# A hybrid decoder step: splitting a mixer's input weights one layer part earlier, and a state update of the decode tokens by matrix products

## The chip, the core and the metric

The kernel runs on one core of one Trainium2 chip. The time is the device time of one execution in microseconds (us); the figure to compare is the median of several executions. The engines are named as in the profile: PE is TensorE (matrix products, with PEld for its weight loads), DVE is VectorE, ACT is ScalarE, POOL is GpSimd, and SP is the sync engine, which here does nothing but issue transfers. Each engine works through its own instructions in a fixed order; a transfer that waits on SP holds up every transfer behind it.

## The reference

A prompt of 1024 new tokens and 8 decode tokens (one new token for each of 8 running sequences) go through two layers. Both sets use the same weights, so the kernel treats them as one block of T = 1032 columns. Layer 0 mixes with a gated DeltaNet and a retention head group, layer 1 with a Mamba-2 (SSD) mixer; each is followed by a squared-ReLU MLP.

```python
for layer in range(DEPTH):                       # DEPTH = 2
    h = rms_norm(x, norm_mix[layer])
    out, states = mixer(h, ...)                  # layer 0: hybrid, layer 1: ssd_mixer
    x = x + out
    a = relu(rms_norm(x, norm_mlp[layer]) @ mlp_w1[layer])      # 1024 -> 4096
    x = x + (a * a) @ mlp_w2[layer]                             # 4096 -> 1024

# ssd_mixer: z, xbc, dt = split(h @ w_in)        # w_in: 1024 x 5152
# xbc = silu(causal_conv(xbc)); xs, B, C = split(xbc)
# 4 groups of 8 heads, head width 64, state size 128, per head and token:
#     S = exp(dt * a) * S + outer(B, dt * xs)     # S: 128 x 64
#     y = S.T @ C + d * xs
```

For the prompt the recurrence is evaluated in blocks. For a decode token it is one step: 8 tokens x 32 heads, each with its own 128 x 64 state, which is read from memory, updated and written back.

## The kernel before

**Products in three passes.** All large products are made in the round-to-fp32r format: each fp32 operand is split into a high part, rounded to fp32r, and the low rest, and `mm3` adds up three products: high weight by high input (line 150), high weight by low input (line 151), low weight by high input (line 152). The input's parts lie in SBUF as `xh`, `xl` (8 tiles of 128 x 1032 each). The weights come as fp32 and are split on the way. `load_w` does it for a piece of 128 x 512: a transfer on SP's queue into `raw` (line 136, three buffers in turn), the norm weight multiplied in on POOL (line 140, `raw<-raw,vec`), the high part by a cast on ACT (line 144, `whi`), the low part by a subtraction on DVE or POOL (line 145, `wlo`). The two parts go to a ring of six buffers, so three pieces are ready or in use at a time.

**A gemm tile** (`products`, `gemm_units`) makes 128 output rows for all 1032 columns: two pieces ("halves"), each used by 3 column blocks of 344 x 4 input tiles x 3 passes = 36 products. The three results are evicted by DVE. A step of the MLP's second product (`gemm_flush`) also uses one piece with 36 products.

**The stages.** The layer-0 mixer and its output projection fill about 0 to 800 us, the first MLP about 800 to 1540, the SSD mixer to about 2330, its output projection, and the second MLP to the end. In an MLP, `up(t)` runs 32 times (one gemm tile each), and after every fourth one `down(b)` adds 4 hidden tiles into the output: eight steps, one for each 128 output rows.

**The SSD mixer** needs 40 gemm tiles of the input weights `wis`: per group 6 that go through the causal convolution (DVE lines 409 to 413, ACT) and 4 gates. While the recurrence of group g runs (`ssd_group`), the gates of group g-1 and the tiles of group g+1 are interleaved. DVE carries evictions, convolution, half of the low parts, and the recurrence; the PSUM tiles of the recurrence (`ps`, two buffers, and `pm`, three) come free when DVE has read them.

**The decode step** (`ssd_decode`, lines 1693 to 1754) holds the state with (head, width) on the partitions and the state size along the free dimension. Per token: ACT scales the four 128 x 128 parts of the state (line 1744), DVE adds a broadcast row B times a per-partition scalar (line 1746, four instructions), POOL multiplies by the broadcast row C (line 1749), DVE reduces (line 1750). PE only broadcasts the rows B and C for two tokens at a time (line 1737, two products of 256 columns), and helps in the preparation (lines 1705, 1720). States come in two at a time on SP's queue (line 1729).

**What sets the order.** The program is written as nested generators; a scheduler then orders each engine's instructions from that, so an instruction can stand ahead of one that is written before it.

## Time and profile before

| | |
|---|---|
| median of 3 executions | 3213.82 us (3210.69 to 3222.39) |
| profiled execution, its own time | 3203.04 us |
| its span, first to last instruction | 3200.8 us |
| PE busy | 3052.8 us, 95% |
| DVE, ACT, POOL busy | 54%, 26%, 39% |
| mean granted PE clock | 0.973 |

The profile gives the busy time of each engine, in total or by windows; the groups of instructions by line, with the mean duration of one and the idle time before them; the waits of an engine with what ended them; and the single instructions in order of time. Two things need care. A PE product is listed with its whole passage, some 320 ns for 344 columns, but the next one starts about 160 ns after it, so durations on PE overlap, and what one costs is read from start to start. And a full fp32 product is listed as two.

### The profile page before, as it was taken

What the parts mean: (1) busy time and instruction counts of PE and PEld (TensorE: products, weight loads), DVE (VectorE), ACT (ScalarE), POOL (GpSimd) and SP (SyncE); (2) the same over time, 40 slices, a digit from 0 to 9 for tenths busy, and PEclk for the clock granted to TensorE, in tenths of its full rate; (3) what the DMA queues carried; (4) which work ended last, traced back from release to release, by engine and by line L of the source; (5) the groups of instructions that cost most, each with busy time, mean ns of one, the idle gap of its engine ahead of it and who ended that gap; (6) DMA issues with size and microseconds to landing.
All of it is one profiled execution on the core that took longest, in us unless ns stands there. A gap on an engine that the chain in (4) does not pass through costs nothing. (4 is left out here: it accounts for less than half of the span.)

```text
span 3200.8 us, 49506 instructions
## 1 busy us (share of the span) xinstructions
PE 3052.8 (95%) x19758; PEld 2918.4 (91%) x19758; DVE 1724.0 (54%) x3189; ACT 841.2 (26%) x1604; POOL 1264.1 (39%) x1234
## 2 busy tenths in 40 slices
PE   7999999989999999999998999999899999999998
PEld 6888888879999999999987988897899999999998
DVE  7664767464333333335888696978635333333334
ACT  3221222214111111114344434343214111111112
POOL 4332324146323323335246556556625233232224
PEclk8899999889999999999999999999999999999999
DMA  3011103133111111111112121222531111111112
GB/s 122 23 44 59 47 22 105 42 132 116 47 47 47 47 48 48 48 47 46 42 52 65 50 84 58 80 74 96 186 109 44 50 47 47 47 47 47 47 49 71
DMA packets 102326, 202.14 MB, mean 63 GB/s; under 512 B 12624, under 2 KB 27728, under 8 KB 102096
## 3 DMA queue, kind: packets, MB, share of 16 engines
q1 hardware_dynamic: 94800, 173.82, 17.4%
q0 software_dynamic: 7296, 25.17, 2.0%
q8 instruction: 155, 2.54, 0.3%
q14 instruction: 75, 0.61, 0.1%
HBM read 157.94 MB, written 38.89 MB: 61 GB/s over the span
## 5 line engine op out<-in xcount | busy, mean ns | idle before, releaser
L150 PE MATMUL pg<-xh,whi 128*128 128x344 f32 x3072 | 1003.2, 327 | 10.8 <-DVE sxc L1460 4.8
L151 PE MATMUL pg<-xl,whi 128*128 128x344 f32 x3072 | 998.2, 325 | 0.0
L152 PE MATMUL pg<-xh,wlo 128*128 128x344 f32 x3072 | 997.2, 325 | 0.7 <-DVE wlo L145 0.7
L150 PEld LDWEIGHTS pg<-xh,whi 128*128 128x128 f32 x3072 | 585.5, 191 | 18.4 <-DVE sxc L1460 5.8
L144 ACT CAST whi<-raw 128x512 fp32r<-128x512 f32 (+2 forms) x443 | 271.6, 613 | 1257.9 <-PE pg L151 859.2
L152 PEld LDWEIGHTS pg<-xh,wlo 128*128 128x128 f32 x3072 | 585.2, 191 | 4.5 <-issue 1.7
L151 PEld LDWEIGHTS pg<-xl,whi 128*128 128x128 f32 x3072 | 584.2, 190 | 4.8 <-issue 2.8
L140 POOL TENSOR_TENSOR raw<-raw,vec 128x512 f32<-128x512 f32 x264 | 306.2, 1161 | 636.8 <-DMA raw<-w 330.0
L151 PE MATMUL pg<-alo,whi 128*128 128x344 f32 (+2 forms) x1476 | 472.4, 320 | 0.0
L152 PE MATMUL pg<-ahi,wlo 128*128 128x344 f32 (+2 forms) x1476 | 472.3, 320 | 0.0
L150 PE MATMUL pg<-ahi,whi 128*128 128x344 f32 (+2 forms) x1476 | 471.5, 319 | 0.0
L1236 DVE TENSOR_TENSOR acc<-acc,pg 128x344 f32<-128x344 f32 x360 | 183.1, 512 | 385.0 <-PE pg L152 384.7
L145 POOL TENSOR_TENSOR wlo<-raw,whi 128x512 fp32r<-128x512 f32 (+2 forms) x179 | 225.2, 1260 | 328.4 <-ACT whi L144 327.4
L145 DVE TENSOR_TENSOR wlo<-raw,whi 128x512 fp32r<-128x512 f32 x264 | 198.4, 752 | 195.6 <-ACT whi L144 185.8
L1227 POOL TENSOR_TENSOR r<-r 128x344 f32<-128x344 f32 x192 | 146.1, 762 | 386.0 <-ACT ahi L1226 337.3
L152 PEld LDWEIGHTS pg<-ahi,wlo 128*128 128x128 f32 x1476 | 277.6, 188 | 0.0
L150 PEld LDWEIGHTS pg<-ahi,whi 128*128 128x128 f32 x1476 | 277.5, 188 | 0.0
L151 PEld LDWEIGHTS pg<-alo,whi 128*128 128x128 f32 x1476 | 277.3, 188 | 0.0
L1228 DVE TENSOR_TENSOR alo<-r,ahi 128x344 fp32r<-128x344 f32 x192 | 135.5, 707 | 254.1 <-POOL r L1227 254.1
L1226 ACT ACTIVATE ahi<-r 128x344 fp32r<-128x344 f32 x192 | 94.7, 493 | 338.8 <-DVE r L1225 338.8
L1225 DVE SCALAR_TENSOR_TENSOR r<-pg,rstd_bc 128x344 f32<-128x344 f32 x186 | 94.9, 510 | 76.7 <-PE pg L152 75.4
L150 PE MATMUL pg<-mhi,whi 128*128 128x344 f32 x408 | 131.5, 323 | 4.9 <-DVE acc L1342 4.9
(540 smaller groups left out, 4439.8 us busy)
## 6 DMA issues: line engine op xcount, KB each, us to landing
raw<-w SPq DMA_DIRECT2D x256, 256.0 KB, 2.6
raw<-wis SPq DMA_DIRECT2D x80, 256.0 KB, 2.7
raw<-wih SPq DMA_DIRECT2D x56, 256.0 KB, 2.9
mraw<-spill SPq DMA_DIRECT2D x17, 512.0 KB, 4.1
accd<-ost SPq DMA_DIRECT2D x48, 172.0 KB, 2.5
acc<-accd SPq DMA_DIRECT2D x16, 516.0 KB, 6.9
dS<-sstate SPq DMA_DIRECT2D x32, 256.0 KB, 2.7
o_sssm<-dS POOLq DMA_DIRECT2D x32, 256.0 KB, 2.3
```

The costliest lines, as they stand in the source:

```text
L140: (norm_eng or nc.gpsimd).tensor_tensor(out=r3, in0=r3, in1=normw.unsqueeze(2).to_broadcast([P, k, n // k]), op=ALU.mult)
L144: nc.scalar.copy(hi[:, :n], raw[:, :n])
L145: (lo_eng or nc.vector).tensor_tensor(out=lo[:, :n], in0=raw[:, :n], in1=hi[:, :n].bitcast(F32), op=ALU.subtract)
L150: t.matmul(ps, lhsT=whi, rhs=xhi, start=start, stop=False)
L151: t.matmul(ps, lhsT=whi, rhs=xlo, start=False, stop=False)
L152: t.matmul(ps, lhsT=wlo, rhs=xhi, start=False, stop=stop)
L1225: nc.vector.scalar_tensor_tensor(out=r, in0=ps, scalar=0.0, in1=self.rstd_bc[:, s], op0=ALU.max, op1=ALU.mult)
L1226: nc.scalar.activation(hi[:, s], r, AF.Square)
L1227: nc.gpsimd.tensor_tensor(out=r, in0=r, in1=r, op=ALU.mult)
L1228: nc.vector.tensor_tensor(out=lo[:, s], in0=r, in1=hi[:, s].bitcast(F32), op=ALU.subtract)
L1236: nc.vector.tensor_tensor(out=s, in0=s, in1=ps, op=ALU.add)
```

## The change

Three parts.

1. **`presplit`**: during the first MLP, the 80 pieces of `wis` are loaded into the `raw` ring, multiplied by the norm weight (POOL, line 164 of the changed kernel), split into `phi` (ACT) and `plo` (DVE) in four buffers of their own, and both parts are written to a buffer in device memory (`split`, 40 x 128 x 4 x 512, line 169). It is a generator: one piece after each `up`, one after each of the first seven steps of each `down`. All `raw` tiles share one ring of three, the presplit's among them.
2. **`load_half`** with a tile number as source: in the SSD mixer the two parts of a half are fetched as they are, by two transfers straight into the `hl` ring (line 176); no engine touches them.
3. **The decode step** keeps the state as (state size) x (head, width). The tokens' values and B rows are transposed to 8 partitions each and laid out in parts (high, high, low against high, low, high) on partitions 0, 32 and 64 of `sxr` and `sbst`; `dBm` masks B by token for four tokens at a time. Per token: POOL scales the state by a factor broadcast beforehand (`egb`), PE makes the outer product in one fp32r product of 512 columns (line 1774), DVE adds it (line 1775), and four full-fp32 products with the state as weights and one column of C give the output (line 1778). ACT copies two tokens' outputs.

The packing of `state_ssm` and the unpacking of its output on the host follow the new layout.

```diff
@@ load_half, presplit
+    def presplit(self, tp):
+        nc, I = self.nc, self.I
+        normw = self.V("mix1", 0, 8)
+        for i in range(40):
+            for kh in range(2):
+                raw = self.wp.tile([P, 512], F32, tag="raw", name="praw", bufs=RAWB)
+                nc.sync.dma_start(raw, I["wis"][i][:, kh * 512:kh * 512 + 512])
+                r3 = raw.rearrange("p (k c) -> p k c", k=4)
+                nc.gpsimd.tensor_tensor(out=r3, in0=r3, in1=normw[...].to_broadcast([P, 4, 128]), op=ALU.mult)
+                hi, lo = [tp.tile([P, 512], F32R, tag="phl", name=nm, bufs=4) for nm in ("phi", "plo")]
+                nc.scalar.copy(hi, raw)
+                nc.vector.tensor_tensor(out=lo, in0=raw, in1=hi.bitcast(F32), op=ALU.subtract)
+                for s, x in enumerate((hi, lo)):
+                    nc.sync.dma_start(self.split[i][:, kh * 2 + s], x.bitcast(F32))
+                yield
     def load_half(self, src, kh, M, normw):
+        if isinstance(src, int):
+            hl = [self.wp.tile([P, 512], F32R, tag="hl", name=nm, bufs=6) for nm in ("whi", "wlo")]
+            for s, x in enumerate(hl):
+                self.nc.sync.dma_start(x.bitcast(F32), self.split[src][:, kh * 2 + s])
+            return hl
@@ mlp
+            pre = iter(()) if last else self.presplit(tp)
...
                 self.gemm_tile(I["w1"][l, t], 128, normw, ev, t == 1)
+                next(pre, None)
...
-                for _ in self.gemm_flush(lambda m: I["w2"][l, b, m], [parts.pop(k) for k in ks], ev):
-                    pass
+                for m, _ in enumerate(self.gemm_flush(lambda m: I["w2"][l, b, m], [parts.pop(k) for k in ks], ev)):
+                    if m < 7:
+                        next(pre, None)
@@ ssd_decode, per pair of tokens
-            pb = self.pm()
             for j in range(2):
-                t.matmul(pb[:, j * 256:j * 256 + 256], lhsT=st["sel8"][...].to_broadcast([16, P]), rhs=rows, start=True, stop=True)
-            bc = small("bc", [P, 2, 2, 128])
-            a.copy(bc, pb.rearrange("p (b k n) -> p b k n", b=2, k=2))
-            for j in range(2):
...
+                gs.tensor_tensor(out=s3, in0=s3, in1=st["egb"][:, b, hs].unsqueeze(2).to_broadcast([P, 8, 64]), op=ALU.mult)
+                po = self.pm()
+                t.matmul(po, lhsT=Bm[:, b % 4], rhs=xr, start=True, stop=True)
+                v.tensor_tensor(out=s, in0=s, in1=po, op=ALU.add)
+                nc.gpsimd.dma_start(self.O["sssm"][g, b], s)
                 for i in range(4):
-                    a.activation(s[:, i], s[:, i], AF.Copy, scale=egf[:, i, b:b + 1])
-                for i in range(4):
-                    v.scalar_tensor_tensor(out=s[:, i], in0=bc[:, j, 0], scalar=xd[:, i, b:b + 1], in1=s[:, i], op0=ALU.mult, op1=ALU.add)
-                nc.gpsimd.dma_start(self.O["sssm"][g, b], cur[j])
-                pr = half("dpr").rearrange("p (i n) -> p i n", i=4)
-                gs.tensor_tensor(out=pr, in0=s, in1=bc[:, j, 1].unsqueeze(1).to_broadcast([P, 4, 128]), op=ALU.mult)
-                v.tensor_reduce(out=y[:, :, b], in_=pr, axis=AX.X, op=ALU.add)
+                    t.matmul(py[:, i * 2 + j:i * 2 + j + 1], lhsT=s[:, i * 128:i * 128 + 128], rhs=C[:, SEQ + b:SEQ + b + 1], start=True, stop=True)
+            a.copy(y[:, :, b0:b0 + 2], py[:, 0:8].rearrange("p (i k) -> p i k", i=4))
```

**The order on SP in the first MLP.** Before, at the passage from the fourth `up` to the first `down`, SP issues the weight pieces one behind the other (line 136 loads; `w1`, `w2` are the MLP's weights):

```order
L136 DMA raw_8140<-w1 128x512
L136 DMA raw_8198<-w2 128x512
L136 DMA raw_8246<-w2 128x512
L136 DMA raw_8294<-w2 128x512
L136 DMA raw_8342<-w2 128x512
L136 DMA raw_8390<-w2 128x512
```

In the changed kernel, in the same `down`, a presplit load (`praw`, line 162) and two writes (line 169, to `split`) stand around every weight piece (line 137):

```order
L162 DMA praw_8447<-wis 128x512
L169 DMA split3_92<-phi_8450 128x512
L169 DMA split3_92<-plo_8451 128x512
L137 DMA raw_8456<-w2 128x512
L162 DMA praw_8504<-wis 128x512
L137 DMA raw_8513<-w2 128x512
L169 DMA split4_93<-phi_8507 128x512
L169 DMA split4_93<-plo_8508 128x512
L162 DMA praw_8561<-wis 128x512
L137 DMA raw_8570<-w2 128x512
```

The writes of a piece stand right behind its own load, so SP waits there until POOL, ACT and DVE have made the parts, and the next weight piece is behind that wait.

**The order on PE at the first pair of decode tokens.** Before, after the last product of a gemm tile come the two broadcasts of line 1737, and the next tile follows (lines 150 to 152):

```order
L152 MATMUL pg_15600<-xh7_78,wlo_15648 128x344
L1737 MATMUL pm_15709<-drows_15589,sel8_14290 128x256 x2
L150 MATMUL pg_15740<-xh0_71,whi_15746 128x344
L151 MATMUL pg_15740<-xl0_79,whi_15746 128x344
L152 MATMUL pg_15740<-xh0_71,wlo_15747 128x344
L150 MATMUL pg_15740<-xh1_72,whi_15746 128x344
```

In the changed kernel (its gemm lines are 151 to 153) the outer product of the first token stands there, then eight gemm products, then the four one-column products of that token and the outer product of the second:

```order
L1774 MATMUL pm_16415<-sxr_15347,dBm_16411 128x512
L151 MATMUL pg_16435<-xh0_71,whi_16438 128x344
L152 MATMUL pg_16435<-xl0_79,whi_16438 128x344
L153 MATMUL pg_16435<-xh0_71,wlo_16439 128x344
L151 MATMUL pg_16435<-xh1_72,whi_16438 128x344
L152 MATMUL pg_16435<-xl1_80,whi_16438 128x344
L153 MATMUL pg_16435<-xh1_72,wlo_16439 128x344
L151 MATMUL pg_16435<-xh2_73,whi_16438 128x344
L152 MATMUL pg_16435<-xl2_81,whi_16438 128x344
L1778 MATMUL pm_16413<-bc_15788,dS_16300 128x1 x4
L1774 MATMUL pm_16424<-sxr_15347,dBm_16411 128x512
L153 MATMUL pg_16435<-xh2_73,wlo_16439 128x344
```

Line 1778 waits for DVE's sum of line 1775, which waits for the product of line 1774; eight gemm products now stand between the two.

**The order on DVE at the same place.** Before, DVE has the low part of a weight piece (line 145), and the decode's line 1746 in between the convolution of the next group (lines 409 to 413):

```order
L1460 TENSOR_TENSOR sxc_15596<-pg_15600,rstd_bc_70 128x344
L145 TENSOR_TENSOR wlo_15972<-raw_15968,whi_15971 128x512
L409 TENSOR_SCALAR x_15240<-sxc_15596,scwh_14286 128x8
L1746 SCALAR_TENSOR_TENSOR dS_15592<-dbc_15712,dxd_15576,dS_15592 128x128
L413 SCALAR_TENSOR_TENSOR x_15240<-sst_15237,scwh_14286,x_15240 128x8
L1746 SCALAR_TENSOR_TENSOR dS_15592<-dbc_15712,dxd_15576,dS_15592 128x128
L413 SCALAR_TENSOR_TENSOR x_15240<-sst_15237,scwh_14286,x_15240 128x8
L1746 SCALAR_TENSOR_TENSOR dS_15592<-dbc_15712,dxd_15576,dS_15592 128x128
L411 SCALAR_TENSOR_TENSOR x_15240<-sxc_15596,scwh_14286,x_15240 128x1024
L413 SCALAR_TENSOR_TENSOR x_15240<-sst_15237,scwh_14286,x_15240 128x8
L411 SCALAR_TENSOR_TENSOR x_15240<-sxc_15596,scwh_14286,x_15240 128x1024
L1746 SCALAR_TENSOR_TENSOR dS_15592<-dbc_15712,dxd_15576,dS_15592 128x128
```

In the changed kernel (convolution lines 432 to 436, evictions line 1495) the low parts are gone and one sum per token, line 1775, is left:

```order
L1495 TENSOR_TENSOR sxc_16304<-pg_16307,rstd_bc_70 128x344
L1495 TENSOR_TENSOR sxc_16304<-pg_16308,rstd_bc_70 128x344
L1775 TENSOR_TENSOR dS_16300<-dS_16300,pm_16415 128x512
L432 TENSOR_SCALAR x_15969<-sxc_16304,scwh_15048 128x8
L436 SCALAR_TENSOR_TENSOR x_15969<-sst_15966,scwh_15048,x_15969 128x8 x2
L1775 TENSOR_TENSOR dS_16302<-dS_16302,pm_16424 128x512
L434 SCALAR_TENSOR_TENSOR x_15969<-sxc_16304,scwh_15048,x_15969 128x1024
L436 SCALAR_TENSOR_TENSOR x_15969<-sst_15966,scwh_15048,x_15969 128x8
L434 SCALAR_TENSOR_TENSOR x_15969<-sxc_16304,scwh_15048,x_15969 128x1024 x2
```

The sum stands right behind the eviction of the gemm tile that ends just before the outer product.

More of the change, by code (lines that the diff above doesn't have):

```diff
@@ L134, in load_w @@
         nc = self.nc
-        raw = self.wp.tile([P, 512], F32, tag="raw", name="raw", bufs=3)
+        raw = self.wp.tile([P, 512], F32, tag="raw", name="raw", bufs=RAWB)
         nc.sync.dma_start(raw[:, :n], src)
@@ L1324, in mlp @@
                 down(HID // 4 - 1)
+                for _ in pre:
+                    pass
                 self.rstd = self.rstd_from()
@@ L1380, in ssm_setup @@
         self.first = self.others()
-        for u, _ in enumerate(self.products(I["wis"][4], 128, normw, self.first)):
+        for u, _ in enumerate(self.products(4, 128, normw, self.first)):
             if u == 1:
@@ L1440, in ssm_setup @@
         nc.vector.tensor_scalar(out=nsel, in0=sel.bitcast(F32), scalar1=-1.0, scalar2=None, op0=ALU.mult)
+        bg = gp.tile([8, 8, 32], F32, tag="hf", name="sbg", bufs=SHF)
+        nc.vector.tensor_tensor(out=bg, in0=g[:8, 8, :].unsqueeze(1).to_broadcast([8, 8, 32]),
+                                in1=self.ident[:8, :8].unsqueeze(2).to_broadcast([8, 8, 32]), op=ALU.mult)
         pt = self.pm()
-        nc.tensor.transpose(pt[:32, 0:8], dt[:8, 8, :], self.ident[:8, :8])
-        nc.tensor.transpose(pt[:32, 8:16], g[:8, 8, :], self.ident[:8, :8])
-        dg = gp.tile([32, 16], F32, name="dgd")
-        nc.scalar.copy(dg, pt[:32, 0:16])
-        st.update(dt=dt, gc=gc, kdf=kdf, egend=egend, grow=grow, sel=sel, nsel=nsel, idr=idr, mmr=mmr, sel8=sel8, dg=dg)
+        nc.tensor.matmul(pt[:, 0:256], lhsT=self.ones[:8, :], rhs=bg.rearrange("p b h -> p (b h)"), start=True, stop=True)
+        egb = gp.tile([P, 8, 32], F32, name="segb")
+        nc.scalar.activation(egb.rearrange("p b h -> p (b h)"), pt[:, 0:256], AF.Exp)
+        xr = gp.tile([P, 512], F32R, name="sxr")
+        bst = gp.tile([P, 128], F32R, name="sbst")
+        for r, n in ((xr, 4), (bst, 1)):
+            nc.vector.tensor_scalar(out=r.rearrange("p (c k) -> p c k", c=n), in0=self.U.unsqueeze(1).to_broadcast([P, n, 128]),
+                                    scalar1=0.0, scalar2=None, op0=ALU.mult)
+        st.update(dt=dt, gc=gc, kdf=kdf, egend=egend, grow=grow, sel=sel, nsel=nsel, idr=idr, mmr=mmr, seq=c3, egb=egb, xr=xr, bst=bst)
         return st
@@ L1595, in ssd_group @@
         selg = selg.rearrange("p h k -> p (h k)")
-        dec = self.ssd_decode(gp, g, x, B, C, st, half, selg)
+        dec = self.ssd_decode(gp, g, x, B, C, st, half)
         grow = st["grow"]
@@ L1691, in ssd_group, with ssd_decode @@
         nc.gpsimd.dma_start(self.O["pssm"][g], S)
-    def ssd_decode(self, gp, g, x, B, C, st, half, selg):
+    def ssd_decode(self, gp, g, x, B, C, st, half):
         nc = self.nc
@@ L1697, in ssd_decode @@
         ident = self.ident
+        hs = slice(g * 8, g * 8 + 8)
         dec = slice(SEQ, T)
-        def small(name, sh, dt=F32):
-            return gp.tile(sh, dt, tag="d" + name, name="d" + name, bufs=1)
-        pd = self.pm()
+        xr, bst = st["xr"], st["bst"]
+        pt = self.pm()
         for i in range(4):
-            t.matmul(pd[:, i * 16:i * 16 + 16], lhsT=selg[:32, i * 128:i * 128 + 128].bitcast(F32), rhs=st["dg"], start=True, stop=True)
-        pd3 = pd[:, 0:64].rearrange("p (i k) -> p i k", i=4)
-        dtf, egf = small("dtf", [P, 4, 8]), small("egf", [P, 4, 8])
-        a.copy(dtf, pd3[:, :, 0:8])
-        a.activation(egf, pd3[:, :, 8:16], AF.Exp)
-        xd = small("xd", [P, 4, 8])
-        v.tensor_tensor(out=xd, in0=x[:, :, dec], in1=dtf, op=ALU.mult)
-        hi, parts = small("hi", [P, 2, 8], F32R), small("parts", [P, 2, 16])
-        for k, src in enumerate((B[:, dec], C[:, dec])):
-            v.tensor_copy(hi[:, k], src)
-            v.tensor_copy(parts[:, k, 0:8], hi[:, k].bitcast(F32))
-            v.tensor_tensor(out=parts[:, k, 8:16], in0=src, in1=hi[:, k].bitcast(F32), op=ALU.subtract)
-        pt = self.pm()
-        for k in range(2):
-            t.transpose(pt[:16, k * 128:k * 128 + 128], parts[:, k], ident)
-        rows = small("rows", [16, 256], F32R)
-        a.copy(rows, pt[:16, 0:256])
-        y = small("y", [P, 4, 8])
+            t.transpose(pt[:8, i * 128:i * 128 + 128], x[:, i, dec], ident)
+        xd = half("dxd")[:8]
+        v.tensor_tensor(out=xd.rearrange("p (h k) -> p h k", h=8), in0=pt[:8].rearrange("p (h k) -> p h k", h=8),
+                        in1=st["dt"][:8, 8, hs].unsqueeze(2).to_broadcast([8, 8, 64]), op=ALU.mult)
+        a.copy(xr[0:8], xd)
+        a.copy(xr[32:40], xd)
+        v.tensor_tensor(out=xr[64:72], in0=xd, in1=xr[0:8].bitcast(F32), op=ALU.subtract)
+        pt = self.pm()
+        t.transpose(pt[:8, 0:128], B[:, dec], ident)
+        a.copy(bst[0:8], pt[:8, 0:128])
+        a.copy(bst[64:72], pt[:8, 0:128])
+        v.tensor_tensor(out=bst[32:40], in0=pt[:8, 0:128], in1=bst[0:8].bitcast(F32), op=ALU.subtract)
+        y = gp.tile([P, 4, 8], F32, tag="dy", name="dy", bufs=1)
         def fetch(b0):
@@ L1759, in build @@
         k = Kern(ctx, tc, I, O)
+        sp = ctx.enter_context(tc.tile_pool(name="split", bufs=1, space=bass.MemoryType.DRAM))
+        k.split = [sp.tile([P, 4, 512], F32, name=f"split{i}") for i in range(40)]
         k.layer(0)
```

28 lines of the change are left out of this document (16 added, 12 removed).

## The prediction

> **What bounds the kernel now.** I read the page's first lines, then busy time by windows cut at the stages, then PE's waits inside the SSD mixer. A windows row has the stretch, its length, the busy time of PE, PEld, DVE, ACT and POOL with the instruction counts, the granted clock, the DMA share and GB/s.
>
> ```profile
> PE 3052.8 (95%) x19758; PEld 2918.4 (91%) x19758; DVE 1724.0 (54%) x3189; ACT 841.2 (26%) x1604; POOL 1264.1 (39%) x1234
> 800.00:1460.00 660.00, 660.00 (x4197) 660.00 (x4196) 230.00 (x411) 117.76 (x208) 203.22 (x207) 1.00 0.16 47
> 1540.00:2330.00 790.00, 732.01 (x4816) 675.55 (x4816) 613.09 (x976) 297.61 (x563) 433.19 (x365) 0.98 0.25 83
> ```
>
> In the first MLP (800 to 1460) PE never pauses, and DVE, POOL and ACT are busy for 35%, 31% and 18%. In the SSD mixer (1540 to 2330) PE is idle for 790 - 732 = 58 us, DVE is busy for 613 of 790 us (78%), POOL for 55%. So work can be taken to the first MLP under cover, and all that removing it from the mixer can win is those 58 us and what the granted clock lost. These are PE's longest waits in the mixer (in total, times, longest):
>
> ```profile
> PE ps L1677 <- DVE x L1667: 10.6, 10, 2.2
> PE ps L1665 <- DVE yi L1674: 9.8, 6, 3.0
> PE pg L150 <- DVE ost L473: 5.6, 4, 2.8
> PE pm L1645 <- DVE selg L1594: 5.2, 1, 5.2
> PE pg L150 <- DVE sxc L1460: 4.8, 4, 1.9
> PE pg L150 <- DVE z L1485: 4.5, 2, 2.5
> PE pg L150 <- DVE acc L1342: 3.2, 1, 3.2
> PE ps L294 <- DVE dg L292: 2.3, 4, 0.7
> ```
>
> Every one ends with DVE: PE is the bound and DVE is what makes it pause. `ost`, `acc` and `dg` (11.1 us) belong to the norms and the output projection, which the change leaves alone. That leaves 58 - 11 = 47 us of waits that it can touch. The pauses cost more than themselves:
>
> ```profile
> 641.00:647.80 6.80, 6.80 (x29) 5.46 (x27) 4.89 (x10) 2.42 (x5) 2.45 (x3) 0.50 0.21 77
> 1743.50:1750.30 6.80, 3.80 (x14) 3.83 (x15) 6.23 (x11) 1.99 (x4) 4.87 (x4) 0.50 0.21 76
> 2050.70:2054.10 3.40, 2.96 (x6) 1.96 (x7) 2.15 (x4) 0.19 (x1) 3.32 (x4) 0.50 0.38 130
> ```
>
> Around the 5.2 us wait for `selg` (1743 to 1750) the granted clock is half. Over the mixer it is 0.98, so (1 - 0.98) x 790 = 16 us go that way.
>
> **PE's own work: more.** The single instructions give start-to-start times.
>
> ```profile
> 1602.31 0.40 PE L1609 MATMUL pm<-smmr,sidr 128*128 128x512 f32 x1
> 1602.54 0.40 PE L1611 MATMUL pm<-sgrow,ssel 128*128 128x256 f32 x2
> 1640.59 1.06 PE L1705 MATMUL pm<-dgd,selg 32*128 32x16 f32 x8
> 1641.72 0.40 PE L150 MATMUL pg<-xh,whi 128*128 128x344 f32 x1
> 1652.78 0.32 PE L151 MATMUL pg<-xl,whi 128*128 128x344 f32 x1
> 1652.94 0.32 PE L152 MATMUL pg<-xh,wlo 128*128 128x344 f32 x1
> 1653.19 0.50 PE L1737 MATMUL pm<-drows,sel 16*128 16x256 f32 x2
> 1653.62 0.43 PE L150 MATMUL pg<-xh,whi 128*128 128x344 f32 x1
> 1653.88 0.32 PE L151 MATMUL pg<-xl,whi 128*128 128x344 f32 x1
> 638.17 1.95 PE L1189 MATMUL pm<-rqm,drS 128*128 128x2 f32 x16
> 639.98 0.27 PE L1007 MATMUL pm<-c,ork 128*48 128x128 f32 x1
> 654.72 1.70 PE L1189 MATMUL pm<-rqm,drS 128*128 128x2 f32 x8
> 656.28 0.63 PE L151 MATMUL pg<-of,whi 128*128 128x344 f32 x1
> ```
>
> A gemm product takes 0.16 us (1652.78 to 1652.94). The old pair of broadcasts: 1652.94 to 1653.88 holds two gemm products (0.32) and the pair, so 0.62 us; 16 pairs are 9.9 us. Lines 1705 and 1720 take 1640.59 to 1641.72, 1.1 us and some 0.1 of delay, in four groups 4.9. Removed: 14.8 us.
>
> Added: line 1778 is 32 tokens x 4 products with one column, state as weights, full fp32. Its like is L1189 (two columns, same weights): 16 records in 639.98 - 638.17 = 1.81 us, 0.113 each, two to a product. So 128 x 2 x 0.113 = 28.9 us. The outer products are 32 of 512 columns at 0.23 (1602.31 to 1602.54): 7.4. Each trip out of the gemm stream costs about 0.19 beside the work (0.09 before and 0.10 after the pair above); by the order there are three trips per pair of tokens, 48 x 0.19 = 9.1. The 20 small transposes at about 0.13 are 2.6. Added 48, **net +33 us**. Lower end: no trip costs, +24. Upper end: one-column products at half clock, 8 records in 1.56 us at 654.72, so 0.195 each and 50 us in place of 29: +54. I take +33, since the trips are there in the rows and the clock is mostly full.
>
> **DVE: less.** Groups in the mixer's window, and one line's spread:
>
> ```profile
> L145 DVE TENSOR_TENSOR wlo<-raw,whi 128x512 fp32r<-128x512 f32 x76 | 63.4, 835 | 14.9 <-ACT whi L144 12.3 <-PE pg L152 2.2
> L1746 DVE SCALAR_TENSOR_TENSOR dS<-dbc,dxd,dS 128x128 f32<-128x128 f32 x128 | 65.0, 555 | 0.0
> L1750 DVE TENSOR_REDUCE dy<-dpr 128x4 f32<-128x512 f32 x32 | 21.8, 682 | 13.7 <-POOL dpr L1749 13.6
> L1715 DVE CAST dhi<-bc 128x8 fp32r<-128x8 f32 x8 | 12.2, 1522 | 0.0
> L1683 DVE TENSOR_TENSOR S<-S,ps 128x512 f32<-128x512 f32 x28 | 19.1, 681 | 8.8 <-POOL S L1682 6.5 <-PE ps L1677 1.7 <-PE pm L1614 0.2
> 1739.93 5.23 DVE L1746 SCALAR_TENSOR_TENSOR dS<-dbc,dxd,dS 128x128 f32<-128x128 f32 x3
> L140 POOL TENSOR_TENSOR raw<-raw,vec 128x512 f32<-128x512 f32 x74 | 95.5, 1291 | 159.4 <-DMA raw<-wis 127.6 <-DVE sxc L1460 7.9 <-DVE dg L292 4.8
> L1746 DVE SCALAR_TENSOR_TENSOR dS<-dbc,dxd,dS x128: 335/344/4708, 1654.6 to 2227.7; 128x128 f32<-128x128 f32 x128
> ```
>
> Away go lines 145, 1746, 1750 and 1715: 63 + 65 + 22 + 12 = 162 us. New are 32 sums from PSUM like L1683, 32 x 0.68 = 22, and about 18 pieces of the masks and parts at up to 0.7, 12. Net -128 us: DVE falls from 613 to some 485 of 790 (61%). POOL loses 95 us of norm products, and its new scaling replaces line 1749; ACT loses 80 casts of line 144 and the scaling of line 1744. Neither is named in PE's long waits, so I book nothing for them. How much of PE's 47 us goes with it? One end is all of it. The other is a third: some waits (the 3.0 us for `yi`) are round trips and not a queue. The `selg` wait is the queue itself: in the 6 us before it ended DVE was at line 1746, which goes (three of them took 5.2 us from 1739.9). I take three quarters, **-35 us**, and half of the clock's 16, **-8**.
>
> At L1746 one form takes from 335 to 4708 ns, so DVE is also held up by something. The Trainium skill (SBUF — State Buffer, "SBUF: two separate sides") says that POOL and a DVE operation with two SBUF inputs share an exclusive port lock, and the second fully waits. The trace agrees as far as the spread goes. By that rule the smaller POOL load would shorten DVE's remaining operations too, by an estimate of 20 us of DVE time, and the total would come out some 4 us lower than by the rows alone.
>
> **New waits.** The one-column products wait for a sum, which waits for the outer product. Between them stand eight gemm products, 8 x 0.16 + 0.23 = 1.5 us; DVE has to finish one eviction (0.5) and the sum (0.68). That nearly fits: 32 x 0.15 = **+5 us** (ends 0 and, with the whole sum uncovered, 22). Behind the waiting product stands the gemm stream.
>
> **The first MLP and SP.** What is moved there, and its prices:
>
> ```profile
> L145 POOL TENSOR_TENSOR wlo<-raw,whi 128x512 fp32r<-128x512 f32 x51 | 65.8, 1290 | 91.9 <-ACT whi L144 91.9
> L144 ACT CAST whi<-raw 128x512 fp32r<-128x512 f32 x102 | 63.5, 623 | 350.8 <-PE pg L151 212.1 <-PE pg L152 133.4 <-POOL raw L140 5.3
> L140 POOL TENSOR_TENSOR raw<-raw,vec 128x512 f32<-128x512 f32 x54 | 56.7, 1051 | 167.3 <-DMA raw<-w 150.4 <-DVE acc L1236 16.9
> L145 DVE TENSOR_TENSOR wlo<-raw,whi 128x512 fp32r<-128x512 f32 x51 | 35.2, 690 | 65.6 <-ACT whi L144 63.2
> raw<-wis SPq DMA_DIRECT2D x80, 256.0 KB, 2.7
> ```
>
> 80 x (1.05 + 0.62 + 0.69) = 189 us over three engines that are two thirds idle there, under a PE that is never idle: 0 on the path. If that cover were gone, all 189 would be too, but each engine has 430 us to spare. The transfers grow from one per piece to 80 loads and 160 writes more, 63 MB in some 700 us, 90 GB/s beside the 47 of the windows row; its DMA share of 0.16 would come to about 0.5, so the engines that move data do not bind either. The queue is the risk. SP stands at a piece's writes until load (2.7), POOL (1.05), ACT (0.62) and DVE (0.69) are through, 5.1 us, about 5.7 with three more issues; a step of `down` is 36 products of 660 / 4197 = 0.157 us, 5.65. It just fits, two pieces are ready ahead (11 us), and an `up` gives time back: I take 0. In the mixer, each half needs two loads, issued when the ring has room, two halves (11 us) ahead of use against 2.7 to land: 0, and if one stood behind a blocked state load, what exceeds 8 us. Before, the same queue could run a further three pieces ahead in `raw`; that reserve is given up, and the state loads (line 1757) now stand between loads that wait for PE.
>
> **Sum.** +33 - 35 - 8 + 5 = -5 us against the profiled execution's 3203 us. Its span is 2.2 us shorter than its time, and the time lies 10.8 us under the median of 3213.8; the difference is carried to the median: **3209 us**.
>
> **Rivals.** *DVE was the whole cause (faster).* All 47 us and all 16 go and no new wait comes: +33 - 63 = -30, so 3184. For it: every row of waits names DVE, which loses a fifth of its work. Against: round trips stay. *The array's clock (slower).* 128 one-column products leave the array nearly empty for 0.9 us, twice in 4 us, 16 times. In the trace the clock fell to half at 641.0, just after the 1.8 us of L1189, for 6.8 us; 6.8 us at half clock cost 3.4, so 16 x 3.4 = 54, less the 8 counted as won: 3213.8 - 5 + 46 = 3255. It decides once the clock in the mixer falls below 0.95. The Trainium skill (TensorE: Matmul & The Clock Gate, "What's actually happening") has a monitor that judges the array's recent busyness in windows of about 3.4 us; the half-clock stretch of 3.4 us at 2050.7 agrees. Against it: in between stand 15 or so gemm products. *The presplit holds up the weight queue (slower).* If the loop at SP takes 6.4 us and not 5.7, 56 steps lose 0.75 each: 42 us, part of it taken back in the `up`s; from about 6.0 on it decides. 3209 + 30 = 3239. *Nothing moves* is in the forecast itself: a third of the relief in place of three quarters gives 3229.
>
> **How the numbers follow.** The measurement tells about 0.5%, 16 us, from no change. Forecast 0.42, DVE rival 0.36, clock 0.11, queue 0.11. The forecast's own range is 3196 to 3229. The range goes to 3170 (all waits gone and PE's work at its lower end: +24 - 63 = -39, 3175) and to 3240 (the queue rival). Nearly all of the forecast's chance is no change, all of the first rival's faster, of the other two slower: faster 0.37, same 0.41, slower 0.22.
>
> **What would show it.** In the new profile: PE in the first MLP still without a pause; line 1778 at 0.11 us a record; DVE in the mixer near 485 us; PE's waits for DVE at a quarter; few waits of line 1778 for line 1775; no gemm product that waits for a `split` load. The forecast is wrong if the mixer shortens by over 16 us, or if a wait for weights or half clock shows in it.

## The result, and the profile after

The changed kernel takes 3268.26 us (median of four executions, 3259.14 to 3269.44), the kernel before 3214.65 us beside it. The ratio is 1.0156, with a 95% interval of 1.0138 to 1.0175: it is slower by about 1.6%. The forecast was 3209 us with a range of 3170 to 3240; the time lies above the range.

In both kernels the instruction order is the same until the first MLP, and from the SSD mixer's output projection on the stages take the same time within 0.4 us (the second MLP's `up` part 674.3 us in both). What differs lies between, read from the start of the first and of the last eviction of each stage in the two profiled executions. The first MLP counts from DVE's turn to its first eviction, so where DVE waits there for the product, that wait (up to 1.2 us) is in it, here and in the runs below:

| stretch | before, us | after, us |
|---|---|---|
| first MLP, from DVE's turn to its first eviction up to the last one of its last `down` | 720.0 | 784.4 |
| from there to the mixer's first eviction | 19.4 | 18.8 |
| mixer, first eviction to its last output | 754.4 | 741.2 |

So the mixer gained 14 us with its setup and the first MLP lost 64. The sum is +51; the medians differ by 54. (The two executions also differ by 15 us ahead of the first MLP, where the order is the same. Over the eleven profiled executions of this study, whose kernels share that part, it took between 795 and 819 us, with no order by the edits; it is not counted to the change.)

The page's first lines of the changed kernel give the busy time of each engine:

```profile
PE 3107.2 (95%) x19994; PEld 2969.2 (91%) x19994; DVE 1650.0 (51%) x3055; ACT 794.8 (24%) x1480; POOL 1247.0 (38%) x1234
```

PE is busy for 54 us more than before (3052.8), though its share is the same 95%. Windows by stage (length, busy time of PE, PEld, DVE, ACT and POOL with their counts, granted clock, DMA share, GB/s) give the whole first MLP, 100 us of it, and the mixer, and below them the same two stages of the kernel before:

```profile
812.00:1596.00 784.00, 738.37 (x4552) 725.35 (x4552) 309.71 (x546) 184.22 (x347) 327.86 (x319) 0.98 0.38 122
1100.00:1200.00 100.00, 93.84 (x588) 92.07 (x586) 39.44 (x68) 21.41 (x39) 40.91 (x40) 1.00 0.41 132
1615.00:2356.00 741.00, 719.35 (x4864) 673.36 (x4862) 480.83 (x742) 209.56 (x356) 315.39 (x271) 0.98 0.32 101
```

```profile
796.60:1516.60 720.00, 717.99 (x4560) 716.95 (x4558) 268.30 (x470) 146.06 (x271) 241.74 (x244) 1.00 0.16 47
1536.00:2290.00 754.00, 700.43 (x4627) 643.97 (x4626) 600.30 (x953) 292.63 (x556) 413.47 (x345) 0.98 0.22 73
```

In the first MLP PE pauses now (738 of 784 us busy; before, 718 of 720), and no engine is the bound: DVE is busy for 40%, POOL for 42%, ACT for 23%. The pauses are 46 us, 44 more than before. The other 20 us are in PE's busy time, with the same products: by the trace's clock records 24 us of the stretch ran at half clock, which makes 12 of the 20. The remaining 8 are not accounted for in full; a product right after a pause is listed longer (0.42 us in place of 0.32 in the stall below). So it is not PE's work that grew; something waits. The waits in that stretch (in total, times, longest):

```profile
PE pg L151 <- DVE r L1250: 24.2, 20, 3.1
PE pg L151 <- DVE acc L1262: 20.4, 16, 5.0
...
DVE plo L167 <- ACT phi L166: 200.6, 64, 5.8
DVE alo L1253 <- POOL r L1252: 132.7, 95, 5.1
...
POOL praw L164 <- DMA praw<-wis: 160.0, 65, 6.5
...
SPq L169 <- ACT phi L166: 318.9, 71, 6.8
SPq L162 <- DVE wlo L146: 83.4, 28, 4.9
SPq L162 <- POOL wlo L146: 42.0, 7, 7.0
```

PE waits for DVE's evictions (`r` in an `up`, `acc` in a `down`) because its three PSUM tiles are not freed. But DVE is not busy: it stands at `plo`, the low part of a piece that is split ahead, and at `alo`. Behind that stand ACT and POOL, and POOL stands 65 times at a piece's norm until the load of the piece has landed. The loads in turn stand on SP, behind the writes of the piece before (line 169, 319 us) and for a buffer of the shared ring (line 162 waiting for the split of one of the MLP's own weights, 125 us).

One stall, in order of time, shows the whole chain (start, duration, engine and line, what is written from what; in brackets the idle time ahead and what ended it):

```profile
1048.38 0.33 SPq L169 DMA_DIRECT2D split<-plo  x1
1049.26 0.45 SPq L162 DMA_DIRECT2D praw<-wis  x1
1051.21 0.51 DVE L1250 SCALAR_TENSOR_TENSOR r<-pg,rstd_bc 128x344 f32<-128x344 f32 x1
...
1054.21 1.04 POOL L164 TENSOR_TENSOR praw<-praw,vec 128x512 f32<-128x512 f32 x1 [3.46 <-DMA praw<-wis]
1055.20 0.76 POOL L1252 TENSOR_TENSOR r<-r 128x344 f32<-128x344 f32 x1
1056.00 0.52 DVE L1253 TENSOR_TENSOR alo<-r,ahi 128x344 fp32r<-128x344 f32 x1 [4.28 <-POOL r L1252]
1056.43 0.51 DVE L1250 SCALAR_TENSOR_TENSOR r<-pg,rstd_bc 128x344 f32<-128x344 f32 x1
1057.00 0.42 PE L151 MATMUL pg<-xh,whi 128*128 128x344 f32 x1 [2.22 <-DVE r L1250]
```

SP issues the piece's load at 1049.3, behind the last write of the piece before and one load of the MLP's own weights (1048.81). POOL stands at its norm until 1054.2. The square `r*r` of the MLP (line 1252) stands behind that norm on POOL although ACT's square of the same `r`, started at 1051.8 and 0.5 long, was the last thing it had to wait for; DVE stands at `alo`, which needs the square; the next eviction (line 1250) stands behind `alo`; and PE, out of PSUM tiles, loses 2.2 us. Following each pause of PE over 0.2 us back in this way gives the same end for at least 36 of 44 us: POOL at a norm, waiting for a load of a piece.

From issue to the finished low part a piece takes 6.5 us on average (80 pieces), and where two norms follow within 9 us of each other, as in a `down`, the mean distance is 7.5 us; a step of a `down` takes 5.65. Seven pieces in eight steps (52 us against 45) cannot keep up with that.

In the mixer DVE is busy for 481 us, as forecast, and PE's waits are few. The longest three in total:

```profile
PE pm L1778 <- DVE dS L1775: 5.1, 4, 1.5
PE pm L1778 <- ACT th L443: 4.6, 3, 2.2
PE ps L1700 <- DVE E L1673: 3.4, 1, 3.4
```

### The profile page after: what moved, and what is told of

Same layout as the page of the kernel before. It is cut to its first block, busy times and chain, and to the rows that moved or that the text cites. A ratio compares the mean times of both kernels' runs of the same rounds, so it can differ in the third digit from the quotient of the medians.

```text
span 3266.3 us, 50233 instructions
## 1 busy us (share of the span) xinstructions
PE 3107.2 (95%) x19994; PEld 2969.2 (91%) x19994; DVE 1650.0 (51%) x3055; ACT 794.8 (24%) x1480; POOL 1247.0 (38%) x1234
## 5 line engine op out<-in xcount | busy, mean ns | idle before, releaser
L151 PE MATMUL pg<-ahi,whi 128*128 128x344 f32 (+2 forms) x1476 | 478.9, 324 | 32.1 <-DVE acc L1262 20.4
L145 ACT CAST whi<-raw 128x512 fp32r<-128x512 f32 (+1 forms) x363 | 220.8, 608 | 828.8 <-PE pg L152 557.5
L141 POOL TENSOR_TENSOR raw<-raw,vec 128x512 f32<-128x512 f32 x184 | 204.3, 1116 | 408.7 <-DMA raw<-w 266.4
L1253 DVE TENSOR_TENSOR alo<-r,ahi 128x344 fp32r<-128x344 f32 x192 | 125.3, 653 | 260.5 <-POOL r L1252 260.5
L146 DVE TENSOR_TENSOR wlo<-raw,whi 128x512 fp32r<-128x512 f32 x184 | 138.9, 755 | 135.6 <-ACT whi L145 131.3
L167 DVE TENSOR_TENSOR plo<-praw,phi 128x512 fp32r<-128x512 f32 x80 | 65.4, 817 | 200.7 <-ACT phi L166 200.6
L164 POOL TENSOR_TENSOR praw<-praw,vec 128x512 f32<-128x512 f32 x80 | 84.9, 1061 | 180.5 <-DMA praw<-wis 162.0
```

What stands on the lines that cost most here:

```text
L141: (norm_eng or nc.gpsimd).tensor_tensor(out=r3, in0=r3, in1=normw.unsqueeze(2).to_broadcast([P, k, n // k]), op=ALU.mult)
L145: nc.scalar.copy(hi[:, :n], raw[:, :n])
L146: (lo_eng or nc.vector).tensor_tensor(out=lo[:, :n], in0=raw[:, :n], in1=hi[:, :n].bitcast(F32), op=ALU.subtract)
L151: t.matmul(ps, lhsT=whi, rhs=xhi, start=start, stop=False)
L164: nc.gpsimd.tensor_tensor(out=r3, in0=r3, in1=normw[:, kh * 4:kh * 4 + 4].unsqueeze(2).to_broadcast([P, 4, 128]), op=ALU.mult)
L167: nc.vector.tensor_tensor(out=lo, in0=raw, in1=hi.bitcast(F32), op=ALU.subtract)
```

## The experiments

Theory Q at the start: the whole loss is the first MLP's, and it comes from SP, which stands at the writes of a piece and so issues the next load late. The runs' ratios below are against the kernel before, on the same chip.

**1. The new decode step alone.**

```diff
-            pre = iter(()) if last else self.presplit(tp)
+            pre = iter(())
...
         if isinstance(src, int):
-            hl = [self.wp.tile([P, 512], F32R, tag="hl", name=nm, bufs=6) for nm in ("whi", "wlo")]
-            for s, x in enumerate(hl):
-                self.nc.sync.dma_start(x.bitcast(F32), self.split[src][:, kh * 2 + s])
-            return hl
+            src = self.I["wis"][src]
```

> The changed kernel with the new decode step alone: no piece is split ahead, and the mixer loads, norms and splits its weights as before. First MLP (from its first eviction to the last one of its last down step) was 720 us before and 784 with the whole change; setup and mixer together were 14 us shorter with the whole change. Theory Q (all of the loss is in the first MLP, where the weight queue on SP stands at the writes of a piece, the pieces come late, and DVE's evictions and POOL's squares stand behind them in their fixed order): the first MLP takes 720 again, the mixer lies between as before and 14 us shorter, total 3198 to 3216. Rival D (the decode step costs: its PE work of +33 us is not paid back): total over 3225, the mixer longer.

Measured: ratio 1.0017 (0.9997 to 1.0037). The first MLP takes 719.9 us, as before: the loss there belongs to the presplit. But the mixer is 7 us longer (761.6), not 0 to 14 shorter: alone, the new decode step wins nothing. The mixer's window, and PE's longest wait in it (lines 1775 and 1772 are the changed kernel's 1778 and 1775):

```profile
1535.00:2296.00 761.00, 727.82 (x4862) 679.72 (x4860) 552.34 (x818) 253.99 (x432) 407.81 (x345) 0.97 0.22 72
```

```profile
PE pm L1775 <- DVE dS L1772: 15.4, 6, 4.1
```

PE is busy for 27 us more than before (728 against 700), its pauses fall from 54 to 33 us, and half of these are the new wait of the one-column products for the state sum. The granted clock fell too, from 0.98 to 0.97: 44 us of this mixer ran at half clock by the trace's clock records, 31 before, so some 7 of the 27 us are clock and not work.

**2. The presplit alone**: the kernel before with `presplit` and the split loads of the change, of which only the lines that call them are shown here, and nothing of `ssd_decode`.

```diff
+            pre = iter(()) if last else self.presplit(tp)
...
+                next(pre, None)
...
-        for u, _ in enumerate(self.products(I["wis"][4], 128, normw, self.first)):
+        for u, _ in enumerate(self.products(4, 128, normw, self.first)):
```

> The kernel before with the split ahead and the split loads alone: the decode step is the old one. Theory Q: the first MLP takes 780 to 790 us as in the changed kernel; the mixer is shorter than before, since DVE loses 63 us of low parts and PE gets no new work: by 10 to 30 us. Total 3214 + 64 - 20 = 3258, between 3245 and 3270. Rival D: the first MLP's loss comes only together with the decode step: total under 3225.

Measured: ratio 1.0097 (1.0077 to 1.0117), 3246 us. The first MLP takes 783.1 us: the whole loss is here without the decode step. The mixer takes 728.6, 26 us less than before. So the split loads win 26 us in the mixer, and the new decode step on top of them costs 12.6 (741.2). The mixer's window:

```profile
1607.00:2336.00 729.00, 691.29 (x4630) 641.94 (x4628) 525.22 (x877) 247.14 (x480) 313.53 (x272) 0.99 0.33 103
```

**3. The writes on ACT's queue.**

```diff
-                    nc.sync.dma_start(self.split[i][:, kh * 2 + s], x.bitcast(F32))
+                    nc.scalar.dma_start(self.split[i][:, kh * 2 + s], x.bitcast(F32))
```

> The changed kernel with one edit: the two writes of a piece are issued by ACT's queue and not by SP's. As many bytes move, the ring of three raw buffers is shared as before, DVE keeps the low part. Theory Q: SP no longer stands at a piece's writes, the next loads are issued as soon as a buffer is free, the wait of ACT for the piece's norm falls from 324 us to under 150, and the first MLP takes 720 to 740 us in place of 784: total 3203 to 3225. Rival R (the shared ring of three holds the pieces up: a piece's load has to wait for the buffer of a weight): first MLP stays over 770, total over 3250. Rival B (the added traffic, 63 MB, or the two engines' access to SBUF slows everything): first MLP stays over 770 as well, but without late pieces: DVE's and POOL's single operations or the landing times are longer.

Measured: ratio 1.0251 (1.0231 to 1.0272); the first MLP takes 818 us, longer than with the writes on SP. Theory Q as stated falls. SP's waits show what takes the place of the writes:

```profile
SPq L137 <- POOL wlo L146: 183.1, 34, 8.3
SPq L137 <- DMA praw<-wis: 181.7, 63, 4.6
SPq L137 <- DVE plo L167: 173.0, 64, 5.8
```

SP now stands at the MLP's own weight loads (line 137), whose buffer in the shared ring is held by a piece that has not landed or has not been split; the next piece's load is queued behind them. PE's pauses still go back to a norm that waits for its load (63 of 68 us). Why it became worse and not only no better isn't shown. ACT's casts now stand behind writes that wait for DVE, but by the trace's records ACT stands at them for 23 us in all (47 times), and no run tells what that costs.

**4. A ring of their own for the pieces.**

```diff
-                raw = self.wp.tile([P, 512], F32, tag="raw", name="praw", bufs=RAWB)
+                raw = tp.tile([P, 512], F32, tag="praw", name="praw", bufs=3)
```

> The changed kernel with one edit: a piece split ahead gets a ring of three buffers of its own. The pieces are no longer paced by the weights: by the written order of the instructions 27 of the 80 stand before the end of the first down step, 67 before the end of the second and all before the third, in place of 12, 25 and 41. Theory Q: SP still stands at the writes, now with some three pieces in the time of one before, so weights come late for PE itself: the loss sits in the first 200 us of the MLP, 40 to 120 us of it, and the rest of the MLP runs without a pause; total 3240 to 3320. Rival R (the shared ring is what makes the pieces late): first MLP 720 to 740, total 3203 to 3225.

Measured: ratio 1.019 (1.017 to 1.0211); the first MLP takes 789.6 us. With nothing that ties a piece to a step, the scheduler packs all 80 into the first 290 us, at 242 GB/s, and the whole loss is there; then PE runs almost without a pause. PE waited for evictions there, as in the other runs, and not for weights as expected. The windows of the two parts:

```profile
819.00:1110.00 291.00, 242.26 (x1400) 233.66 (x1400) 150.07 (x217) 83.78 (x150) 161.21 (x146) 0.93 0.75 242
1110.00:1480.00 370.00, 368.48 (x2341) 368.20 (x2342) 130.45 (x231) 66.21 (x117) 116.67 (x117) 1.00 0.16 50
```

A ring of its own without a pace is thus no cure. Followed back, 32 of the 50 us of PE's pauses end at a norm that waits for its load, and 17 at a split part whose buffer was still being written out:

```profile
POOL praw L164 <- DMA praw<-wis: 68.3, 30, 5.9
DVE plo L167 <- DMA split<-plo: 23.3, 11, 3.9
```

What the changed kernel and the runs 2 to 4 have in common is the late load, whatever makes it late. That gave theory L: the engines work through a fixed order, so the load has to have landed before the norm's turn comes; the same work with early loads should cost nothing.

**5. The loads ahead, the pace kept.** A piece's norm takes its weights from a small tile that depends on a result of its step, so a piece cannot be split before its step; its ring of three lets the load run ahead. (The last two lines stand in `up` and in `down`.)

```diff
-                raw = self.wp.tile([P, 512], F32, tag="raw", name="praw", bufs=RAWB)
+                raw = tp.tile([P, 512], F32, tag="praw", name="praw", bufs=3)
...
+                nw = tp.tile([P, 4], F32, tag="nw", name="nw", bufs=2)
+                nc.vector.scalar_tensor_tensor(out=nw, in0=self.pace, scalar=0.0, in1=normw[:, kh * 4:kh * 4 + 4], op0=ALU.mult, op1=ALU.add)
-                nc.gpsimd.tensor_tensor(out=r3, in0=r3, in1=normw[:, kh * 4:kh * 4 + 4].unsqueeze(2).to_broadcast([P, 4, 128]), op=ALU.mult)
+                nc.gpsimd.tensor_tensor(out=r3, in0=r3, in1=nw.unsqueeze(2).to_broadcast([P, 4, 128]), op=ALU.mult)
...
+                self.pace = hi[:, 0:4].bitcast(F32)
...
+                    self.pace = acc[m][:, 0:4]
```

> The changed kernel with the pieces' loads taken ahead and the pace kept: the pieces have a ring of three of their own, and the norm of a piece takes its weights from a 128x4 tile that DVE makes from the norm weights and a result of the step it belongs to (times 0), so a piece cannot be split before its step (9, 23, 38, 53, 67, 80 pieces by the end of each down step, against 12, 25, 41, 56, 69, 80), while its load is free to run up to three pieces ahead. All bytes, norms, casts, subtractions and writes stay, 80 small DVE operations come on top. Theory L (every stall goes back to POOL, which stands at a piece's norm until the piece's load lands; the load is issued too late, for the write ahead of it on SP or for the buffer of the shared ring): POOL's wait for these loads falls from 160 us to under 20, PE's waits in the first MLP from 45 us to under 8, the first MLP to 720 to 730 us, total 3200 to 3215. Rival B (63 MB more traffic and the two engines' access to SBUF): first MLP over 765. Rival P (more work on DVE, POOL and ACT makes the evictions late, whenever the loads come): over 750.

Measured: 3200.7 us, ratio 0.9951 (0.9934 to 0.9968). The first MLP takes 722.1 us with all 80 pieces in it; the mixer is that of the changed kernel (741.6). The first MLP's window, and the waits in it that answer to those shown of the changed kernel:

```profile
799.00:1521.00 722.00, 719.03 (x4556) 716.31 (x4555) 358.72 (x630) 190.30 (x349) 326.75 (x320) 1.00 0.41 133
```

```profile
PE pg L151 <- DVE acc L1265: 2.4, 7, 0.4
...
POOL praw L166 <- DVE nw L165: 36.8, 29, 2.4
...
DVE plo L169 <- ACT phi L168: 17.8, 25, 1.4
```

The bytes, the norms, the casts, the subtractions and the writes are those of the changed kernel, and the traffic per time (133 GB/s against 122) and POOL's busy time (327 us against 328) are not smaller. What differs is that the load comes earlier (from its issue to the norm 21.9 us pass on average, against 3.5) and that a piece is split no sooner than its step. POOL no longer waits for these loads. The rivals B (traffic) and P (more work) fall; theory L holds. Run 4 had the own ring without the pace; run 8 has the pace without the lead.

**6. The same with the old decode step**: the edit of run 5 made in the kernel of run 2.

> As the run before, with the old decode step. Theory L: first MLP 720 to 730 us, and the mixer is the one with split loads alone, some 26 us shorter than before from the end of the MLP to the last output of the mixer: total 3180 to 3198, faster than both kernels. If the new decode step gains on its own, this is slower than the run before; by the runs so far (the mixer 7 us longer with the new decode step alone, 26 us shorter with the split loads alone, 14 us shorter with both) it is 10 to 15 us faster than that run. Rivals B and P: 3225 to 3245.

Measured: 3190.9 us, ratio 0.9914 (0.9891 to 0.9938): faster than the kernel before and 2.4% faster than the changed kernel. Of the kernels that make every output it is the fastest of the study. The mixer takes 725.1 us, 16.5 less than with the new decode step. The windows of the first MLP and the mixer:

```profile
809.00:1531.00 722.00, 719.02 (x4556) 716.34 (x4555) 360.01 (x629) 190.27 (x349) 326.48 (x320) 1.00 0.41 133
1550.00:2275.00 725.00, 689.87 (x4627) 640.44 (x4625) 523.40 (x877) 247.25 (x480) 315.03 (x272) 0.99 0.33 103
```

**7. The writes left out** (the mixer then loads and splits its own weights, by the same edit of `load_half` as in run 1).

```diff
-                for s, x in enumerate((hi, lo)):
-                    nc.sync.dma_start(self.split[i][:, kh * 2 + s], x.bitcast(F32))
```

> The changed kernel without the 160 writes of the parts; the pieces are loaded and split in the first MLP as before, but what is split is not used, and the mixer loads and splits its own weights. The shared ring of three stays. What it tells: how much of the loss is SP standing at writes and how much is the ring. If the writes ahead of the loads make them late: first MLP 720 to 735. If the ring does (as with the writes on ACT, where SP stood at buffers): 765 to 785. Traffic falls by two thirds of the added, so rival B expects 735 to 745. The mixer as with the new decode step alone, 7 us longer than before; total 3220 to 3240 if the writes are it, 3265 to 3285 if the ring is.

Measured: 3275.6 us, ratio 1.0185 (1.0155 to 1.0216). The first MLP takes 765.5 us: without any write on SP 45 of the 64 us remain, and a load is still issued only 2.9 us before its norm. So the stand at the writes is not the larger part. SP stands at loads for buffers of the shared ring, many of them held by a piece, and POOL at the norms (last line):

```profile
SPq L137 <- DVE plo L167: 198.4, 78, 2.8
SPq L137 <- DMA praw<-wis: 191.1, 78, 3.9
SPq L162 <- DVE wlo L146: 88.0, 35, 5.0
SPq L162 <- POOL wlo L146: 68.9, 42, 5.2
...
POOL praw L164 <- DMA praw<-wis: 118.3, 70, 4.4
```

That points to the shared ring. It is not isolated: SP waits for buffers of that ring in the kernel before as well, where its loads run ahead and PE loses nothing.

**8. The paced kernel with one buffer in place of three** (`bufs=1` for `praw`).

> The paced kernel with one size changed: the pieces' own ring holds one buffer in place of three. The order on SP is the same, but a piece's load can be issued only when the piece before it has been split. Lead theory (what helped is that loads run ahead of their step): a load is issued some 2.4 us after the step's result (norm 1.05, cast 0.62, subtraction 0.69), stands behind two writes (0.8) and lands 3.1 us later, 6.3 us against 5.65 of a down step: late by 0.7 us in each, so POOL waits for the loads again for 40 us or more, and the first MLP takes 730 to 760 us; total 3210 to 3240. Pace theory (what helped is that the split of a piece is tied to its step, and the load need not be ahead): first MLP 722 us as with three, total 3195 to 3205.

Measured: 3235.2 us, ratio 1.007 (1.0042 to 1.0099). The first MLP takes 754.9 us: 33 us of the loss come back with this one size. The pace alone is not enough; the load has to be ahead. (Against the changed kernel it is still 30 us shorter, so of the 62 us between that and run 5 the lead takes back 33, and the pace with a buffer of its own 30.) Followed back, 20 of the 25 us of PE's pauses end at a norm that waits for its piece's load. The first MLP's window, and POOL's and PE's waits in it:

```profile
807.60:1561.50 753.90, 728.37 (x4553) 715.62 (x4554) 361.88 (x629) 186.03 (x349) 322.56 (x319) 1.00 0.40 128
```

```profile
POOL praw L166 <- DMA praw<-wis: 89.1, 29, 5.5
...
PE pg L151 <- DVE acc L1265: 24.9, 36, 1.5
```

**9. The price of the one-column products.**

```diff
-                for i in range(4):
+                for i in range(1):
                     t.matmul(py[:, i * 2 + j:i * 2 + j + 1], lhsT=s[:, i * 128:i * 128 + 128], rhs=C[:, SEQ + b:SEQ + b + 1], start=True, stop=True)
-            a.copy(y[:, :, b0:b0 + 2], py[:, 0:8].rearrange("p (i k) -> p i k", i=4))
+            a.copy(y[:, :, b0:b0 + 2], py[:, 0:2].unsqueeze(1).to_broadcast([P, 4, 2]))
```

> The paced kernel with three of the four one-column products of each decode token left out (96 of 128; the output of the token is then not complete). What is measured is the price of these products in place. By the rows (two records of 0.113 us each) 96 x 2 x 0.113 = 21.7 us of PE work go, so the mixer, 741.6 us from its first eviction to its last output with all of them, gets 18 to 24 us shorter, and the total falls to 3177 to 3183. If the products cost half clock as well (0.195 us a record): 37 us shorter, total 3163. If they stand in PE's idle time and a wait takes their place: less than 10 us shorter, total over 3190.

Measured: 3182.9 us, ratio 0.9915 (0.9883 to 0.9947). The mixer is 21.6 us shorter than in run 5 (720.0 against 741.6), as the rows gave it; PE is busy for 25.8 us less than in the same stretch of run 5 (719.0). The mixer's window:

```profile
1551.00:2271.00 720.00, 693.27 (x4670) 648.69 (x4668) 481.47 (x743) 209.34 (x356) 314.41 (x272) 0.98 0.32 104
```

25.8 us for 96 products of two records are 0.134 us a record, against 0.113 in the forecast; at that price all 128 cost some 34 us of PE, an estimate that counts what they cost around them too. They are on the path.

## Why the prediction was wrong, point by point

**The first MLP: 0 forecast, 64 us measured. This is the step that failed.** The sentence was "80 x (1.05 + 0.62 + 0.69) = 189 us over three engines that are two thirds idle there, under a PE that is never idle: 0 on the path". The work did lie there under cover: run 5 does all of it in 722 us. But the idle time of an engine with a fixed order can be used only by an instruction that is ready. A norm whose load is late does not leave POOL idle for others; it stops POOL (3.5 us in the stall shown, with the next square ready for 2 of them), and the MLP's squares and DVE's evictions behind it.

**SP's loop: 5.7 us forecast, 7.5 measured.** The prediction did name the queue as the risk, and summed a piece as load 2.7, POOL 1.05, ACT 0.62, DVE 0.69. Measured from issue to the end of the low part: 6.5 us. The load takes 3.1 in place of 2.7, and the norm starts 3.5 after the issue; between the engines some 0.4 us are lost; DVE needs 0.82 on average. Then come the issues on SP and the wait for a buffer of the ring, 1 us together. A comparison of 5.7 with 5.65 with nothing to spare was booked as 0 and should have been booked with a price.

**"Two pieces are ready ahead (11 us), and an `up` gives time back".** This is true of the MLP's weights, and PE never waited long for a weight. It does not hold for the pieces split ahead: each of them is loaded just before it is needed, and the shared ring keeps it so. The prediction gives that sharing no price: the reserve of `raw` that it gives up is the mixer's. Without the writes, with the ring still shared, 45 of the 64 us remain (run 7).

**The queue rival (3239, chance 0.11)** came nearest in its place and its sign. Its formula, steps times the excess of the loop, gives 56 x (7.5 - 5.65) = 104 us with the measured loop (91 with the 49 steps of a `down` that the 80 pieces fill), against 64 measured; that the `up`s give back the rest fits, but no run shows it. But what it saw queued behind SP's stand were PE's weights. What really stood there was the work of POOL and DVE, and a cure at SP's writes, which follows from that rival, made it worse (run 3).

**The mixer: -5 us in the sum, -13.2 measured (-13.8 with its setup).** PE's own work was forecast +33: its busy time is +28.1 against the kernel with the presplit alone (run 2) and +27.4 with the decode step alone against the kernel before (run 1), of which some 5 and 7 us are half clock. The one-column products came out dearer (34 against 29, by run 9), and all the rest of the sum, +4 in the forecast, at -6. Against the kernel before it is only +18.9, because in run 2 PE's busy time is 9 us less than before for the same products; that was not foreseen. The clock makes 7 of the 9: 17 us of that mixer ran at half clock, 31 before. The relief by DVE was forecast as -35, with +5 of new waits: PE's pauses fell from 53.6 to 21.7 us, by 32. The new wait of line 1778 for line 1775 is 5.1 us, as said. DVE was forecast at some 485 us and has 481, so the further 20 us that the port lock was to save did not show. The clock was to give 8 us; it stays at 0.98 (27 us at half clock, 31 before) and gives under 2. So the sum missed by 8 us with errors in both directions: less new work on PE, less help by the clock.

**The rival of the array's clock (3255, chance 0.11)** fails in its size: the granted clock in the mixer is 0.98 before and after, above the 0.95 from which it was to decide, though the total comes nearer to it than to any other. A total that fits is no evidence for its mechanism. A small part of it may be real: both mixers with the split loads alone (runs 2 and 6) spent 17 us at half clock, the changed kernel's 27, and with the decode step alone it is 44 against 31, so 5 to 7 us in place of 54. But four more profiled runs with the changed kernel's mixer range from 17 to 31 us, and with three quarters of the one-column products left out (run 9) it is 24; that these products are the cause is not shown. **The rival of DVE as the whole cause (3184)** is not borne out in the mixer either: of the 47 us of pauses that could be touched, and not only of those, 32 went on balance, and the clock gained under 2.

**The split loads in the mixer, no wait forecast:** right, no wait of PE for one is in the mixer's list. What the sum could not show, since it gave one relief for both parts: the split loads alone win 26 us (run 2), and the decode step on top of them costs 12.6 (the changed kernel against run 2) to 16.5 us (run 5 against run 6). Its 28 us of PE's busy time are more than the pauses that it removes (37.7 us in run 2, 21.7 in the changed kernel).

What stays open: why the writes on ACT's queue lose another 34 us, how much of the loss is the shared ring's, and some 8 us of PE's busy time in the first MLP.

## What to carry to other kernels

Work that is moved under an idle engine needs more than idle time: in a fixed order, one operand that lands late (3.5 us in the stall shown) stops everything behind it on that engine, and on the engines that wait for it. So look at what stands behind each moved instruction, put its load ahead of its turn with a ring of its own, and tie the work (not the load) to the step that is to cover it. When a move has two parts, time them apart: here one won 26 us, the other lost 7 to 16, and a stall elsewhere hid both.

## What the runs showed of the hardware

The first MLP carried the 80 pieces at a DMA share of 0.41 and 133 GB/s without slowing PE: PE was busy for 719 of 722 us in run 5, and the granted clock was 1.00.

In the runs here, pauses of PE cost clock when they were long. In the first MLP of the changed kernel half clock came five times, 24 us in all, each time within 5 us of the start of a pause of 1.9 to 5.0 us; five other pauses of 1.9 to 3.1 us had no such stretch behind them. The stall shown above, with its 2.2 us, is followed by one:

```profile
1058.40:1061.80 3.40, 3.40 (x14) 3.40 (x13) 0.52 (x1) 0.62 (x1) 0.54 (x1) 0.51 0.78 213
```

In run 8 no pause was longer than 1.5 us, and 25 us of them left the granted clock at 1.00. Where the pauses were densest (run 4, 819 to 1110 us) it fell to 0.93.

One DVE instruction of line 1746 in the kernel before took 4.7 us where most take 0.34. It began at 1739.9; POOL ran an operation on SBUF from 1740.3 to 1741.6 and a second from 1742.1 to 1744.5, and the DVE instruction ended 0.2 us after the second. That fits an engine that has to wait until the other has finished; no run here varies it alone.

The load of 256 KB that took a median of 2.7 us from issue to landing in the kernel before takes 3.1 in the first MLP of the changed kernel (122 GB/s), and 2.7 with the writes left out (run 7, 74 GB/s).
